# When the convolution taps of a mixer trunk stand in VectorE's queue: taps held back longer, gates spread out, transposed chunks used later, norm steps later

## The chip, the cores and the metric

One core of one Trainium2 chip runs the kernel. The metric is device time in microseconds (us) of one execution. The engines in play are TensorE (PE for its matmuls, PEld for its weight loads), VectorE (DVE), ScalarE (ACT), GpSimd (POOL) and SyncE (SP). Each takes its instructions in the order in which they stand in its queue, so an instruction that waits holds up everything behind it on that engine. For this kernel a difference of about 0.3% is what can be told from no change.

## The reference, cut to what matters

Two layers (DEPTH = 2) run over 256 tokens of width 2048. Each layer normalises x, multiplies it with one wide input projection, feeds three branches from it, and merges them:

```
h = rms_norm(x, norm_w);  proj = h @ w_in
qa, ka, va, za, qi, ki, wi, ub, zb, qc, kc, vc, zc, gates = split(proj)
y_a = (dsa_attention(rope(qa), rope(ka), va, rope(qi), rope(ki), wi, top_k=64) * silu(za)) @ w_a_out
y_b = (conformer_conv(ub) * silu(zb)) @ w_b_out   # GLU, depthwise causal conv of 31 taps, LayerNorm, swish
y_c = (stick_breaking_attention(qc, kc, vc) * silu(zc)) @ w_c_out
x   = x + (g_a*y_a + g_b*y_b + g_c*y_c) @ w_out   # g = sigmoid(gates)
```

After the second layer a final RMSNorm gives the output. All is float32. The 1024 convolution channels are 8 blocks of 128, so a layer has 8 x 31 = 248 tap instructions of 128x256 elements.

## The kernel before, in words

**Weight units.** Every large product is fed by weight units of half a megabyte, mostly 2 x 128 rows by 512 columns (`load_unit`, L193). A unit is loaded into `raw` (4 buffers) by a DMA that SP issues; ACT rounds it to `wh` (`high`, L216; the cast of L218); DVE forms the rest `wl = raw - wh` (`low`, L220; the subtraction of L222). Both `wh` and `wl` have 3 buffers. PE then does 8 matmuls with `wh` and 4 with `wl` for a unit (L232). So DVE may run ahead of PE by less than three units, and whatever else DVE does must fit between two subtractions of L222, or PE waits for `wl`.

**Shapes of chunk.** `chunk_N` (L332) makes 512 output columns by tokens in 8 units; `chunk_T` (L235) makes two heads of features by tokens in 4 units (the 16 index query heads, called QI here, take 8 such chunks, and `rope`, L383, works on each). `chunk_F` (L286) is a `chunk_N` whose result is turned by `turned` (L254): DVE transposes 32x32 blocks, POOL issues four DMAs to a scratch tensor `z` and, two units later, one DMA back into `zy`; the result is used `later` units after the chunk.

**Order.** The program is written in one order with priorities, and a list scheduler in the recording layer orders each engine's instructions from it. `high`, `low` and the loads have high priority. Several devices place side work between units: `waiting` holds convolution taps in items of one or two, and `drain` (L174) puts one item after each `low`, tied to stand behind that subtraction, unless `hold[0]` is set; `flush` (L185) emits all that is left in `waiting` at once, tied to nothing; `stages` holds generators (index scores, attention, stick breaking, the convolution's norm) of which `background` (L156) advances one per unit, and `finish` runs them out; `pending` holds the turned results and `settle` runs them out.

**Taps.** `use_u` (L672) copies a turned half of the GLU output (4 channel blocks) to `yT` on ACT and calls `taps` (L661), which puts the taps of that half in `waiting`: channel blocks two at a time, their taps alternating, so that neighbours in the queue write different rows of `cv`. `hold[0]` is set before the QI chunks (L698) and cleared behind them (L702). `tap` (L420) is one VectorE instruction, L424 for the first tap of a block and L426 for the other 30; each of these reads and writes its block of `cv`.

**The layer's sequence.** Two chunks of the first product with the squares and the norm's factor beside them (`chunk_first`, `start_0`, `start_1`, `follow`); the second half of the GLU; QI, KI, VA with the index weights, KA; QA (two `chunk_F` with `rope_F`) and QC (two) with the index scores and the choice of the top 64 as stages; KC, VC with attention as stages; the gate ZA; then for the branches in the order A, C, B four rounds of a gate chunk (8 units) and an output chunk (4 units). The gates ZC and ZB stand just ahead of branches C and B. `conv_norm` (L909) starts in branch C at j = 2, after a `flush`: it sums `cv` over the channels (L914, L915), PE forms the mean (L918), DVE subtracts it (L921), ACT squares, DVE sums again (L924, L925), PE forms the variance (L928), and so on; it gives 3 units between the first two steps and 6 before the variance. Last come the output product and, for layer 0, the transposes of the last x tile for the next layer (`x_turn`, L435, called at L633).

Of the kernel before, what the change touches and what calls it, by code (L numbers as in the profile page):

```python
# [14 lines left out]
P = 128  # L15
S = 256
NT = S // P
# [7 lines left out]
TOPK = 64  # L25
TAPS = 31
PRE = 2
LATER = 9
URGENT = 10 ** 6
PAD = TAPS - 1  # L30
EPS = 1e-6
# [17 lines left out]
def trunk(ctx: ExitStack, tc: tile.TileContext, x, w_in, xt, w_a, w_b, w_c, w_out,  # L49
# [235 lines left out]

    def chunk_F(w, c0, act, nk, use, later=LATER):  # L286
        turned(chunk_N(w, [(c0, 512)], act, nk), use, later)
# [121 lines left out]
    def gate(c0, o, b, w, hx):  # L409
        def use(k, y):  # L410
            sg = sigmoid_of(y)
            yield 1
            nc.vector.tensor_mul(y, y, sg)  # L413
            nc.vector.tensor_mul(y, y, blocks(o[:, k:k + 4, :]).rearrange("p k u i -> p u k i"))
            split(blocks(hi(b, k, 4)), blocks(lo(b, k, 4)), by_feature(y))

        for k in range(0, KC, 4):
            chunk_F(w, c0 + k * P, hx, KD, partial(use, k), LATER - 1)

    def tap(yT, cv, pr, c, q):  # L420
        wq = pr[:, P_CW + c * TAPS + q:P_CW + c * TAPS + q + 1]
# [52 lines left out]
    for layer in range(DEPTH):  # L474
# [8 lines left out]
        with tc.manual_schedule(engines={nc.vector.engine}), ExitStack() as order:  # L483
# [11 lines left out]
            def low_x(i):  # L495
                k = i * 2
                xs = xT[k // KC][:, k % KC:k % KC + 2, :]
                nc.vector.tensor_sub(lo(hx, k, 2), xs, hi(hx, k, 2).bitcast(F32))
# [8 lines left out]

            def follow(k0):
                u = k0 // 2
                if u:  # L510
                    scale_x(u - 1)
                if u > 1:
                    low_x(u - 2)
                if u == 3:
                    for t in range(NT):
                        nc.scalar.activation(sgs[t], ga[t], AF.Sigmoid, scale=state["r"][:, t:t + 1])
                return advance_units(k0)[0], None if u else lambda: spread(state["dg"])

            todo = [(k, 2, seg[0]) for k in range(0, KD, 2)] + [(k, 2, seg[1]) for k in range(0, KD, 2)]
            loaded, ready = [], []  # L520
# [72 lines left out]
            def start_0(k0):  # L593
                if k0 == 0:
                    load(2)
                    warm_sqrt()
                    load_x(2)
                    load()
                    load_x(4)
                    load()  # L600
                    ps = mm_tile()
                    for _ in range(10):
                        nc.tensor.matmul(ps[:, :P], idle, idle, start=True, stop=True)
                    nc.vector.tensor_copy(loaded[0][1], loaded[0][0])
                    x_high(0)
                    high(loaded[1])
                    x_low(0)
                    for u in loaded[:2]:
                        low(u)
                    ready.extend(loaded[:2])  # L610
                    del loaded[:2]

                    def between():
                        step(2)
                        load_x(6)
                        load()

                    return next_unit(0) + next_unit(1), between
                if k0 < 14:
                    step(k0 + 2)  # L620
                    if k0 < 10:
                        load_x(k0 + 6)
                    load()
                    return next_unit(k0), None
                sq = state["sq"]
                state["sum"] = state["sq2"][:, :S]
                nc.vector.tensor_add(sq[:, :2 * S], sq[:, :2 * S], sq[:, 2 * S:])
                nc.vector.tensor_add(state["sum"], sq[:, :S], sq[:, S:2 * S])
                return advance_units(k0)[0], total_square

            def start_1(k0):
                if k0 == 2:
                    x_parts(x_turn(tail), xn, 12, nw, 4)  # L633
                if k0 == 14:
                    state["r"] = rsqrt_mean(ssq_total(ssq), D)
                    state["dg"] = diag_cols(state["r"])
                return advance_units(k0)
# [8 lines left out]
            order.close()  # L646
            ua = chunk_first(ux, follow)
        with tc.high_priority():
            scale_x(KD // 2 - 1)
            low_x(KD // 2 - 2)  # L650
            low_x(KD // 2 - 1)
        if layer == 0:
            for d, v in ((upper_r, upper), (ones_r, ones)):
# [34 lines left out]
        with tc.high_priority():  # L688
            for t in range(NT):
                nc.vector.tensor_mul(sgs[t], a[t], sgs[t])  # L690
        turned(sgs, partial(use_u, 1), LATER + 2)


        qi = [slot(F32R).rearrange("p a b -> p (a b)").rearrange("p (h t) -> p h t", t=P) for _ in range(2)]
# [4 lines left out]
        for h in range(0, NIH, 2):  # L699
            rope(chunk_T(w, O_QI + h * P, 256, hx, KD, TOPK), qi0[:, h * TOPK:h * TOPK + P].rearrange("p (h t) -> p h t", h=2),  # L700
                 tuple(v[:, h:h + 2, :] for v in qi))
        hold[0] = False  # L702
        kiT = sp.tile([P, 1, S], F32, tag="kiT", bufs=1, name=nm("kiT"))
        rope(chunk_T(w, O_KI, P, hx, KD), kiT)
        with tc.high_priority():
# [89 lines left out]
        for h in range(0, NH, 4):  # L795
            chunk_F(w, O_QC + h * P, hx, KD, partial(use_q, h))
        finish()

        def attend(t, c, qaT=qaT, kaT=kaT, va=va, bias=bias):
            n = (t + 1) * P  # L800
# [34 lines left out]
                start(attend(t, c))  # L835


        kcT, vc = slot(), slot()

        def use_k(h, y, kcT=kcT):  # L840
            nc.scalar.copy(blocks(kcT[:, h:h + 4, :]), by_feature(y))
# [1 line left out]

        for h in range(0, NH, 4):
            chunk_F(w, O_KC + h * P, hx, KD, partial(use_k, h))
        vcr = vc.rearrange("p a b -> p (a b)").rearrange("p (t f) -> p t f", t=NT)
        for j in range(2):
            a = chunk_N(w, [(O_VC + j * 512, 512)], hx, KD)
# [52 lines left out]
                                 lb[:, 512 + q * P:512 + (q + 1) * P], start=False, stop=True)  # L901
            nc.scalar.copy(qcT[:, h0:h0 + 2, :], po[:, :512].rearrange("p (h t) -> p h t", h=2))

        ga = parts(KC)
        gate(O_ZA, qaT, ga, w, hx)
        for h0 in range(0, NH, 2):
            start(stick(h0))

# [38 lines left out]
            yield 0  # L947

        for b in (0, 2, 1):
            if b == 2:  # L950
                finish()
                settle()
                gc = parts(KC)
                gate(O_ZC, qcT, gc, w, hx)
            if b == 1:
                finish()
                settle()
                gb = parts(KC)
                gate(O_ZB, cv, gb, w, hx)
                mx = parts(KD)  # L960
            gx = ga if b == 0 else gc if b == 2 else gb
            for j in range(4):
                if b == 2 and j == 2:
                    finish()
                    flush()
                    start(conv_norm())
                g = chunk_N(w, [(O_G + b * D + j * 512, 512)], hx, KD)
                sg = [ev() for _ in range(NT)]
                with tc.high_priority():
                    for t in range(NT):  # L970
                        nc.scalar.activation(sg[t], g[t], AF.Sigmoid)  # L971
                if j == 0:
                    settle()
                y = chunk_N((w_a, w_b, w_c)[b][layer], [(j * 512, 512)], gx, KC)
                with tc.high_priority():
                    for t in range(NT):
                        dst = mg[j // 2][:, j % 2, t, :]
                        if b == 0:
                            nc.vector.tensor_mul(dst, y[t], sg[t])
                        else:  # L980
                            nc.vector.tensor_mul(sg[t], y[t], sg[t])  # L981
                            nc.vector.tensor_add(dst, dst, sg[t])  # L982
                if b == 1:
                    turned([mg[j // 2][:, j % 2, t, :] for t in range(NT)], partial(use_m, j))


        last = layer == DEPTH - 1
# [21 lines left out]
        def emit_x(xc, accs, q, c0, ts):  # L1009
# [10 lines left out]
            else:  # L1020
                x_squares([xc[:, t, :] for t in ts], ssq, q, ts)
                if q < 3:
                    turned([xc[:, t, :] for t in ts], partial(x_parts_F, xn, c0 // P, nwn), LATER - 1,
                           t4() if q == 1 else None)

        def store_x(xc, c0):
# [103 lines left out]
```

## Time and profile before

| what | value |
|---|---|
| median of 3 runs | 2044.97 us (2043.63 to 2049.26) |
| the profiled execution's own time | 2046.64 us |
| its span, first to last instruction | 2044.9 us |
| mean granted TensorE clock | 0.999 |
| PE busy | 2030.1 us, 99% of the span |
| DVE busy | 1492.4 us, 73% |
| ACT busy | 1039.8 us, 51% |

The profile shows one execution. The span lies 1.7 us under that execution's time. The ends of matmuls are modelled, so a busy PE may still be paced by gaps between matmul starts: where PE is 99% busy, the distance from one group's start to the next, and the number of matmuls in a stretch, say more than the busy time. In the timeline view a row is: start, us, engine, line and operation, output<-input and shapes, and how many were merged; the square bracket gives the idle time before it and what ended that.

### The profile page before, as it was taken

The numbers are of one execution on the slowest core, as the hardware profiler recorded it, in microseconds if no ns is written. First come the engines' busy times: TensorE is split into PE (matmuls) and PEld (weight loads), VectorE is DVE, ScalarE is ACT, GpSimd is POOL, SyncE is SP. The second block draws the span as 40 slices with busy tenths as digits, with TensorE's granted clock in tenths as the row PEclk, the third lists the DMA queues.
The fourth block names the chain that finished last, engine by engine and source line by source line (L and its number), as shares of the span: only waits on it lengthen the run. The fifth ranks groups of instructions, "written<-read, shape, count | busy, mean of one in ns | idle before, by whom it ended". The sixth has DMA issues, their size and how long they took to land.

```text
span 2044.9 us, 26156 instructions
## 1 busy us (share of the span) xinstructions
PE 2030.1 (99%) x9680; PEld 1716.5 (84%) x9680; DVE 1492.4 (73%) x2020; ACT 1039.8 (51%) x1223; POOL 119.4 (6%) x199
## 2 busy tenths in 40 slices
PE   9999999999999999999999999999999999999998
PEld 7899888888888888888888998888888888878887
DVE  8678988688778675655775799886886676656565
ACT  7465445466444454444554654554664444544443
POOL 0100011010000001010100001110100000011000
PEclk9999999999999999999999999999999999999999
DMA  7777587675567667776877776776756776677774
GB/s 258 230 243 213 161 244 210 200 221 167 178 199 228 185 198 227 241 234 213 295 212 231 229 198 178 238 212 192 222 163 180 212 215 195 187 235 244 244 225 152
DMA packets 246528, 435.03 MB, mean 213 GB/s; under 512 B 19712, under 2 KB 69888, under 8 KB 246272
## 3 DMA queue, kind: packets, MB, share of 16 engines
q1 hardware_dynamic: 231632, 389.32, 63.1%
q0 software_dynamic: 13104, 40.91, 6.5%
q10 hardware_dynamic: 1664, 3.15, 0.4%
q8 instruction: 75, 1.23, 0.2%
q14 instruction: 53, 0.43, 0.1%
HBM read 408.67 MB, written 24.64 MB: 212 GB/s over the span
## 4 chain that ended last, share of the span: by engine, by line
PE 92%; DVE 3%; DMA 2%; issue 1%; ACT 1%; POOL 0%; SPq 0%; DVEq 0%; ACTq 0%; POOLq 0%
PE acc L232 89%; DMA zy<-z 1%; DVE wl L222 1%; DMA z<-zt 1%; PE mm L771 1%; PE mm L804 1%; ACT wh L218 0%; PE mm L829 0%; DVE s L426 0%; PE mm L898 0%; PE mm L862 0%; DMA raw<-in_w_in_dram 0%; DVE sc L730 0%; POOL z L268 0%; PE mm L821 0%
## 5 line engine op out<-in xcount | busy, mean ns | idle before, releaser
L232 PE MATMUL acc<-wh,s 128*128 128x512 f32 (+2 forms) x5248 | 1284.5, 387 | 3.3 <-ACT wh L218 3.3
L222 DVE TENSOR_TENSOR wl<-raw,wh 128x1024 fp32r<-128x1024 f32 (+2 forms) x729 | 875.2, 1206 | 400.5 <-ACT wh L218 399.6
L218 ACT CAST wh<-raw 128x1024 fp32r<-128x1024 f32 (+2 forms) x728 | 756.5, 1043 | 785.6 <-PE acc L232 532.4
L232 PEld LDWEIGHTS acc<-wh,s 128*128 128x128 f32 x5248 | 970.7, 188 | 200.0 <-ACT wh L218 5.3
L232 PE MATMUL acc<-wl,s 128*128 128x512 f32 (+2 forms) x2624 | 692.4, 386 | 0.7 <-DVE wl L222 0.7
L232 PEld LDWEIGHTS acc<-wl,s 128*128 128x128 f32 x2624 | 486.9, 188 | 102.6 <-DVE wl L222 4.1
L426 DVE SCALAR_TENSOR_TENSOR s<-yT,cst,s 128x256 f32<-128x256 f32 x480 | 216.1, 476 | 0.5
L268 POOL DMA_DIRECT2D z<-zt x152 | 88.8, 591 | 1639.4 <-DVE zt L265 1491.3
L232 PE MATMUL acc<-s,wh 128*128 128x384 f32 (+1 forms) x608 | 125.6, 348 | 0.0
L232 PEld LDWEIGHTS acc<-s,wh 128*128 128x128 f32 x608 | 104.3, 189 | 3.2
L232 PEld LDWEIGHTS acc<-s,wl 128*128 128x128 f32 x608 | 79.1, 191 | 0.9
L232 PE MATMUL acc<-s,wl 128*128 128x192 f32 (+1 forms) x608 | 79.4, 273 | 0.0
L366 ACT CAST s<-zy 128x1024 fp32r<-128x1024 f32 x20 | 21.0, 1050 | 46.6 <-DMA zy<-z 29.1
L367 DVE TENSOR_TENSOR s<-zy,s 128x1024 fp32r<-128x1024 f32 x20 | 24.4, 1218 | 27.7 <-ACT s L366 27.7
L273 POOL DMA_DIRECT2D zy<-z x39 | 28.0, 719 | 201.3 <-DMA z<-zt 112.4
L265 DVE STREAM_TRANSPOSE zt<-acc 128x512 f32<-128x512 f32 x48 | 34.0, 708 | 7.2 <-PE acc L232 7.2
L981 DVE TENSOR_TENSOR ev<-acc,ev 128x512 f32<-128x512 f32 x32 | 22.0, 687 | 19.1 <-PE acc L232 19.1
L391 DVE TENSOR_TENSOR ev<-ev,cst 128x384 f32<-128x384 f32 (+2 forms) x20 | 11.1, 557 | 25.0 <-ACT ev L389 24.9
L406 ACT ACTIVATE t<-zy 128x1024 f32<-128x1024 f32 x12 | 12.7, 1061 | 29.5 <-DMA zy<-z 29.5
L413 DVE TENSOR_TENSOR zy<-zy,t 128x1024 f32<-128x1024 f32 x12 | 14.6, 1220 | 16.4 <-ACT t L406 16.4
L971 ACT ACTIVATE ev<-acc 128x512 f32<-128x512 f32 x48 | 26.3, 590 | 0.0
L982 DVE TENSOR_TENSOR s<-s,ev 128x512 f32<-128x512 f32 x32 | 21.8, 682 | 0.0
(206 smaller groups left out, 822.5 us busy)
## 6 DMA issues: line engine op xcount, KB each, us to landing
raw<-in_w_in_dram SPq DMA_DIRECT2D x555, 512.0 KB, 3.9
raw<-in_w_out_dram SPq DMA_DIRECT2D x64, 512.0 KB, 4.9
zy<-z POOLq DMA_DIRECT2D x39, 512.0 KB, 5.2
z<-zt POOLq DMA_DIRECT2D x152, 128.0 KB, 4.4
raw<-in_w_a_dram SPq DMA_DIRECT2D x32, 512.0 KB, 3.9
raw<-in_w_c_dram SPq DMA_DIRECT2D x32, 512.0 KB, 4.7
raw<-in_w_b_dram SPq DMA_DIRECT2D x32, 512.0 KB, 5.4
raw<-in_w_in_dram SPq DMA_DIRECT2D x16, 256.0 KB, 3.0
```

The costliest lines, as they stand in the source:

```text
L218: newest_parts[0] = nc.scalar.copy(u[1], u[0])
L222: newest_parts[1] = sub = nc.vector.tensor_sub(u[2], u[0], u[1].bitcast(F32))
L232: newest[0] = nc.tensor.matmul(o, lhsT, rhs, start=start, stop=stop, skip_group_check=True)
L265: nc.vector.transpose(tmp[:, t].rearrange("p b k i -> p k b i"), src.rearrange("p (k b c) -> p k b c", b=4, c=32))
L268: nc.gpsimd.dma_start(z[:, :, :, a, :].rearrange("t b c e -> c (t b) e"), tmp[a * 32:(a + 1) * 32].rearrange("c t b k i -> c (t b) (k i)"))
L273: nc.gpsimd.dma_start(y.rearrange("p (t a) k i -> p t (a k i)", t=n), z.rearrange("t b c a e -> (b c) t (a e)"))
L366: nc.scalar.copy(h, src)
L367: nc.vector.tensor_sub(l, src, h.bitcast(F32))
L426: nc.vector.scalar_tensor_tensor(o, yT[:, c, q:q + S], wq, o, op0=ALU.mult, op1=ALU.add)
L971: nc.scalar.activation(sg[t], g[t], AF.Sigmoid)
L981: nc.vector.tensor_mul(sg[t], y[t], sg[t])
L982: nc.vector.tensor_add(dst, dst, sg[t])
```

## The change

It has these parts.

1. **Taps.** `hold[0] = False` moves from behind the QI chunks to behind the `finish()` after the QC chunks, so `drain` gives out no taps in between.
2. **Later uses.** LATER goes from 9 to 11. A turned chunk is used two units later, but for the merged tiles and x tiles, whose `later` is lowered by two so that it stays, and `use_u(1)`, which stays at 11. `gate` uses 10 and 12.
3. **Gates spread out.** The gate ZA moves from behind VC to between KC and VC, with a `finish()` ahead of it; ZC moves into branch A at j = 3; ZB moves into branch C at j = 3, behind a `finish()`. `flush` and the start of `conv_norm` move from branch C, j = 2, to j = 1.
4. **Norm steps later.** In layer 0 the square sum's product (`total_square`) moves from the last unit of the first chunk into the first unit of the second; `spread`, `scale_x`, `low_x` and the sigmoid of `ga` move one unit later in both layers; in layer 1 the transposes of the last x tile move from k0 = 2 to k0 = 6.

```diff
-LATER = 9
+LATER = 11
...
-            chunk_F(w, c0 + k * P, hx, KD, partial(use, k), LATER - 1)
+            chunk_F(w, c0 + k * P, hx, KD, partial(use, k), LATER + 1 if k else LATER - 1)
...
-                if u:
-                    scale_x(u - 1)
                 if u > 1:
-                    low_x(u - 2)
-                if u == 3:
+                    scale_x(u - 2)
+                if u > 2:
+                    low_x(u - 3)
+                if u == 4:
...
-                return advance_units(k0)[0], None if u else lambda: spread(state["dg"])
+                root = total_square if layer == 0 else None
+                return advance_units(k0)[0], root if u == 0 else (lambda: spread(state["dg"])) if u == 1 else None
...
-                return advance_units(k0)[0], total_square
+                return advance_units(k0)
...
-                if k0 == 2:
+                if k0 == 6:
                     x_parts(x_turn(tail), xn, 12, nw, 4)
...
-        turned(sgs, partial(use_u, 1), LATER + 2)
+        turned(sgs, partial(use_u, 1))
...
-        hold[0] = False
         kiT = sp.tile([P, 1, S], F32, tag="kiT", bufs=1, name=nm("kiT"))
...
         finish()
+        hold[0] = False
...
             chunk_F(w, O_KC + h * P, hx, KD, partial(use_k, h))
+        finish()
+        ga = parts(KC)
+        gate(O_ZA, qaT, ga, w, hx)
+        vc = slot()
...
-        ga = parts(KC)
-        gate(O_ZA, qaT, ga, w, hx)
...
-            if b == 2:
-                finish()
-                settle()
-                gc = parts(KC)
-                gate(O_ZC, qcT, gc, w, hx)
             if b == 1:
-                finish()
-                settle()
-                gb = parts(KC)
-                gate(O_ZB, cv, gb, w, hx)
                 mx = parts(KD)
...
-                if b == 2 and j == 2:
+                if b == 0 and j == 3:
                     finish()
+                    gc = parts(KC)
+                    gate(O_ZC, qcT, gc, w, hx)
+                if b == 2 and j == 1:
                     flush()
                     start(conv_norm())
+                if b == 2 and j == 3:
+                    finish()
+                    gb = parts(KC)
+                    gate(O_ZB, cv, gb, w, hx)
...
-                    turned([mg[j // 2][:, j % 2, t, :] for t in range(NT)], partial(use_m, j))
+                    turned([mg[j // 2][:, j % 2, t, :] for t in range(NT)], partial(use_m, j), LATER - 2)
...
-                    turned([xc[:, t, :] for t in ts], partial(x_parts_F, xn, c0 // P, nwn), LATER - 1,
+                    turned([xc[:, t, :] for t in ts], partial(x_parts_F, xn, c0 // P, nwn), LATER - 3,
```

The scheduler's order of the changed program can be read without running it. In VectorE's queue of layer 0, between the 43rd and the 51st subtraction L222 (in the QI chunks; wl marks such a subtraction, counted as unit 43, 44 and so on, "tap" stands for L424 or L426, the numbers for other lines, which are those of the kernel before):

```
unit 43 wl | tap x2 | unit 44 wl | 293 | tap x3 | 391 392 | unit 45 wl | 401 398 | tap x2 | 367 | tap x2 |
unit 46 wl | tap x6 | unit 47 wl | tap x6 | unit 48 wl | 293 | tap x4 | 391 392 | unit 49 wl |
401 398 | tap x2 | 367 | tap x2 | unit 50 wl | tap x2 | unit 51 wl
```

These are 31 taps: one L424 and 30 L426, neighbours tied by a semaphore to each other: the taps of one whole channel block. In the program before there is no tap at this place. The same stands in layer 1. Around the start of `conv_norm` the changed order of VectorE is (E marks the unit whose matmuls stand just ahead of the mean product L918 in PE's queue):

```
tap x4 | wl of E | tap x3 | wl of E+1 | tap x2 | 914 | wl of E+2 | 915 | 921 | wl of E+3 | 921 | wl of E+4 | 924 924 | wl of E+5 | 925
```

and PE's: unit E but for its last matmul, 918, that matmul, units E+1, E+2 and E+3, one matmul of unit E+4, 928. The last 31 taps, which stand from nine units ahead of E to E+2, are again of one block. In the program before the last tap stands three units ahead of the first L914, and L918 stands 18 units behind the second.

More of the change, by code (lines that the diff above doesn't have):

```diff
@@ L648, in trunk @@
         with tc.high_priority():
-            scale_x(KD // 2 - 1)
-            low_x(KD // 2 - 2)
+            for i in (2, 1):
+                low_x(KD // 2 - i - 1)
+                scale_x(KD // 2 - i)
             low_x(KD // 2 - 1)
@@ L835, in trunk @@
                 start(attend(t, c))
-        kcT, vc = slot(), slot()
+        kcT = slot()
         def use_k(h, y, kcT=kcT):
```

## The prediction

> **What bounds the kernel now.** I read the page's busy times first, then PE's waits, then the windows view, then the timelines of the stretches that the change touches.
>
> ```profile
> span 2044.9 us, 26156 instructions
> PE 2030.1 (99%) x9680; PEld 1716.5 (84%) x9680; DVE 1492.4 (73%) x2020; ACT 1039.8 (51%) x1223; POOL 119.4 (6%) x199
> PEclk9999999999999999999999999999999999999999
> ```
>
> PE is busy for 99% of the span at the full granted clock, and the change adds and removes no matmul. So it can only fill PE's gaps or open new ones. Where are the gaps? The windows view gives each stretch's length, then busy time and instruction count of PE, PEld, DVE, ACT and POOL:
>
> ```profile
> 242.00:275.00 33.00, 32.18 (x138) 24.98 (x137) 31.83 (x61) 14.02 (x15) 3.05 (x5) 1.00 0.68 208
> 1255.00:1288.00 33.00, 31.81 (x136) 24.78 (x135) 31.41 (x61) 13.99 (x14) 3.06 (x5) 1.00 0.70 211
> 560.00:593.00 33.00, 33.00 (x147) 27.36 (x146) 23.29 (x34) 13.64 (x14) 0.00 (x0) 1.00 0.67 195
> 535.00:680.00 145.00, 145.00 (x641) 120.10 (x640) 103.28 (x129) 63.69 (x64) 6.10 (x10) 1.00 0.69 206
> ```
>
> Undisturbed, PE puts 147 matmuls through in 33 us, and over 145 us one in 145 / 641 = 0.226 us. Where the index scores' top 64 are chosen, with taps beside them, it is 138 and 136, and DVE is busy for 31.8 and 31.4 of 33 us. 138 x 0.226 = 31.2 and 136 x 0.226 = 30.8 us are work; 1.8 and 2.2 us are lost, **4.0 us** over both layers. The other gaps that the change touches are small:
>
> ```profile
> PE mm L589 <- DVE t L628: 1.2, 1, 1.2
> ```
>
> ```profile
> 1022.74 0.33 PE L440 MATMUL mm<-cst,t 128*128 128x128 f32 x1
> 1023.34 0.98 PE L440 MATMUL mm<-cst,t 128*128 128x128 f32 x7 [0.27 <-DVE t L1013]
> ```
>
> PE waits 1.2 us for the square sum in layer 0, and the second transpose of the last x tile starts 0.60 us behind the first where the seven others take 0.98 together: 0.5 us lost.
>
> **The change part by part: what goes.** The same window for L426 alone (DVE's time, then taps):
>
> ```profile
> 242.00:275.00 33.00, 7.80 (x17) 1.00 0.68 208
> ```
>
> Without these 7.8 us DVE's 31.8 of 33 become 24, so its lateness goes. Part of the same loss is another wait that the later uses remove: the rotation's copy L374 holds ACT until its chunk has landed, with the next cast behind it.
>
> ```profile
> 270.59 1.05 ACT L374 COPY t<-zy 64x1024 f32<-64x1024 f32 x1 [5.14 <-DMA zy<-z]
> 1284.46 1.05 ACT L374 COPY t<-zy 64x1024 f32<-64x1024 f32 x1 [4.62 <-DMA zy<-z]
> ```
>
> Two units more are about 5.4 us, as long as those waits. So I take the 4.0 us as gone. The square sum's product gets 2.7 us more of matmuls ahead of it and loses its 1.2; the factor behind it then has as many matmuls as before to hide under, and the scaling of x is one unit later, still ahead of the units that read it. The transposes of x move 7 us behind their data: 0.5 goes. Sum of gains: **5.7 us**. The gates' moves put each gate 20 units ahead of its use, which costs nothing; POOL's order of transfers stays. Attention's last two steps now stand with one unit between them (the new `finish()`); by the subtractions that stand ahead of theirs in DVE's queue they are ready about when PE asks: 0 to 1 us a layer, taken as 0.
>
> **What comes, first place: the QI chunks.** The changed order has 31 taps of one block between units 43 and 51. They come from the `flush`: draining starts later and stops earlier, so about 61 taps are left there; `flush` ties them to nothing, and the scheduler puts the last block at the first place where its input exists. That input is ACT's copy L673. The stretch as it stands:
>
> ```profile
> 114.13 1.04 ACT L673 COPY yT<-zy 128x1024 f32<-128x1024 f32 x1
> ```
>
> ```profile
> 117.52 1.03 PE L232 MATMUL acc<-s,wl 128*128 128x192 f32 x8
> 118.38 1.59 PE L232 MATMUL acc<-s,wh 128*128 128x384 f32 x8
> 119.81 1.03 PE L232 MATMUL acc<-s,wl 128*128 128x192 f32 x8
> ```
>
> ```profile
> 112.03 3.49 DVE L222 TENSOR_TENSOR wl<-raw,wh 128x1024 fp32r<-128x1024 f32 x3
> 115.58 0.56 DVE L293 TENSOR_TENSOR ev<-acc,ev 128x384 f32<-128x384 f32 x1
> 117.73 0.56 DVE L391 TENSOR_TENSOR ev<-ev,cst 128x384 f32<-128x384 f32 x1 [1.59 <-ACT ev L389]
> 118.20 0.55 DVE L392 TENSOR_TENSOR ev<-ev,cst 128x384 f32<-128x384 f32 x1
> 118.67 1.22 DVE L222 TENSOR_TENSOR wl<-raw,wh 128x1024 fp32r<-128x1024 f32 x1
> 119.81 0.28 DVE L401 TENSOR_TENSOR s<-ev,ev 128x128 f32<-128x128 f32 x1
> 120.01 0.42 DVE L398 TENSOR_TENSOR ev<-ev,ev 128x256 f32<-128x256 f32 x1
> 120.90 0.43 DVE L367 TENSOR_TENSOR s<-ev,s 128x256 fp32r<-128x256 f32 x1 [0.47 <-ACT s L366]
> 121.24 3.49 DVE L222 TENSOR_TENSOR wl<-raw,wh 128x1024 fp32r<-128x1024 f32 x3
> ```
>
> PE takes a unit each 2.29 us (117.52 to 119.81). DVE's costs from start to start are 1.14 for a subtraction, 0.47 for L293, L391 and L392, 0.20 for L401, 0.34 for L398 and L367. A tap's cost depends on what stands ahead of it:
>
> ```profile
> 207.79 1.52 DVE L777 SCALAR_TENSOR_TENSOR sc<-t,sm,sc 128x256 f32<-128x256 f32 x3
> 270.34 1.27 DVE L426 SCALAR_TENSOR_TENSOR s<-yT,cst,s 128x256 f32<-128x256 f32 x3
> ```
>
> Three taps on alternating blocks take 1.27 us, 0.40 from start to start; three L777, same operation and size, each reading what the last one wrote, 1.52, thus 0.52. The trace has no chain of taps; I take L777's pace, the same dependence, so n taps in a row cost 0.52(n - 1) + 0.40. [...]
>
> The copy ends at 115.17; two taps and the subtraction of unit 44 end at about 117.2, 2.6 us ahead of PE's need at 119.81. Then DVE needs, unit by unit: 45: 0.47 + 1.44 + 0.94 + 1.14 = 3.99 (the three taps fill the 1.59 us of idle time); 46: 0.54 + 0.92 + 0.34 + 0.92 + 1.14 = 3.86; 47 and 48: 3.00 + 1.14 = 4.14 each; 49: 0.47 + 1.96 + 0.94 + 1.14 = 4.51; 50: 3.86. That is 24.5 against PE's 6 x 2.29 = 13.7. Less the 2.6 ahead, PE loses 8.2 us. Units 53 and 54, with the next rotation and DVE not yet ahead again, add about 0.7: **8.9 us a layer, 17.8 in all**. At 0.40 a tap it is 5.9 a layer, and with 0.52 for every tap 9.9; I keep both ends.
>
> **Second place: the start of the convolution's norm.** The mean's product L918 now stands in PE's queue before DVE can have its input, and everything of PE is behind it.
>
> ```profile
> 659.44 0.69 DVE L981 TENSOR_TENSOR ev<-acc,ev 128x512 f32<-128x512 f32 x1 [1.31 <-PE acc L232]
> 660.05 1.22 DVE L222 TENSOR_TENSOR wl<-raw,wh 128x1024 fp32r<-128x1024 f32 x1
> ```
>
> ```profile
> 663.78 1.07 PE L232 MATMUL acc<-wl,s 128*128 128x512 f32 x4
> 664.68 1.98 PE L232 MATMUL acc<-wh,s 128*128 128x512 f32 x8
> 666.50 1.07 PE L232 MATMUL acc<-wl,s 128*128 128x512 f32 x4
> ```
>
> ```profile
> 649.73 2.04 DVE L914 TENSOR_REDUCE t<-s 128x256 f32<-128x1024 f32 x1
> 704.29 2.34 DVE L921 TENSOR_TENSOR s<-s,mm 128x1024 f32<-128x1024 f32 x2
> 707.68 3.94 DVE L924 TENSOR_REDUCE t<-t 128x256 f32<-128x1024 f32 x2
> 712.67 0.42 DVE L925 TENSOR_TENSOR t<-t 128x256 f32<-128x256 f32 x1
> ```
>
> A unit takes PE 2.72 us here (663.78 to 666.50). At the end of an output chunk DVE waits for PE (L981) and then delivers the third unit's `wl` at 661.3, 5.2 us ahead of 666.5; with three taps more ahead of L981 I put the lead at 3.7. The units after it cost DVE 2.4 to 3.1 us (a subtraction and 2 to 4 chained taps, 0.92 to 1.96) against 2.72, so it stays near 3.7 up to unit E. From there DVE needs three taps 1.44, a subtraction 1.14, two taps 0.92, L914 1.96, a subtraction 1.14, L915 0.34: 6.9 us. PE reaches L918 0.7 us into unit E's `wl`: it waits 6.9 - 3.7 - 0.7 = 2.5 us. From the mean to the variance DVE needs L921, subtraction, L921, subtraction (4 x 1.14), two L924 (3.9), a subtraction and L925: 10.3 us with a third for the mean product; PE has three units and two matmuls, 8.8: 1.5 us. Together **4.0 us a layer, 8.0 in all**; with a lead of 5.2 it is 2.5, with none 7.7.
>
> **Sum.** 17.8 + 8.0 - 5.7 = +20.1 us. On the profiled execution: 2044.9 + 20.1 = 2065.0 for the span, 2046.64 + 20.1 = 2066.7 for its own time. That execution lies 1.7 us above the median 2044.97, so a median of runs comes out at **2065.0 us**, 1.0% slower.
>
> **The rivals.**
>
> *Faster: DVE swallows the early taps.* The mechanism is the idle time of DVE in the QI chunks, which decides if it and the lead hold all 31 taps; then the norm's product must also find its input.
>
> ```profile
> 100.00:136.00 36.00, 36.00 (x252) 36.00 (x252) 25.73 (x36) 23.68 (x32) 2.77 (x5) 1.00 0.82 248
> ```
>
> Of 36 us 10.3 are idle, 29%; in the eight units that is 5.2 us, and the lead before the copy is 119.81 - 115.52 = 4.3. These 9.5 us hold 18 taps in a chain. All 31 would need 16, at 0.40 still 12.4. If it did, only the gains would be left: 2044.97 - 5.7 = 2039.3. Chance 3%.
>
> *No change.* At the least, 12.4 - 9.5 = 2.9 us a layer are lost in QI, and if the norm's wait were all covered, 5.8 us of loss meet 5.7 of gain: 2045. Chance 6%.
>
> *Slower by less.* Chained taps at 0.40: 2 x 5.9 + 2 x 2.5 - 5.7 = +11.1: 2056. Chance 14%.
>
> *Slower by more: the clock drops.* PE would now idle in bursts; a clock halved for 16 us behind them (seven units of 2.29) would cost 8 us more a layer: 2081. Against it: with 1.8 and 2.2 us lost around 242 and 1255 the clock stayed at 1.00. [...] Chance 5%.
>
> **How the numbers follow.** The forecast has the remaining 72%. Its bounds: low, QI at 5.9 and the norm at 2.5 (+11.1, 2056); high, 9.9 and the norm's 5 (+24.1, 2069), with up to 2 for attention's last steps and 2.5 more for a norm with no lead. I give 2054 to 2074. A difference of 0.3% (6.1 us) is about what can be told from no change: slower beyond it 72 + 14 + 5 = 91%, within it 6%, faster 3%.
>
> **What would show each step right or wrong.** In the changed profile: the QI stretch near 120 to 140 us with DVE busy throughout, PE waiting for `wl` some 1 to 2 us in each of about five units, and the same 1.0 ms later; taps in a chain 0.52 apart; waits of PE at the mean and variance products (2.5 and 1.5); 147 matmuls in 33 us where the top 64 are chosen; no wait at L589. I am wrong if PE keeps its 2.29 us a unit there, or if the wait at the mean's product is absent.

## The result, and the profile after

The changed kernel takes 2061.88 us (median of 6, 2060.94 to 2062.61) against 2045.18 for the kernel before (median of 6, 2043.37 to 2049.26): 1.0079 times, 95% interval 1.0066 to 1.0092, 16.7 us slower. The forecast was 2065.0. The profiled span grows from 2044.9 to 2060.8 us. In the changed file some lines have moved: the mean product is L922 (was L918), the variance product L932 (L928), their inputs L919 and L929; L222, L232 and L426 stay.

The page's first rows, then PE's waits (in total, times, longest):

```profile
span 2060.8 us, 26151 instructions
PE 2035.9 (99%) x9680; PEld 1721.7 (84%) x9680; DVE 1504.4 (73%) x2020; ACT 1042.1 (51%) x1223; POOL 119.2 (6%) x199
```

```profile
PE acc L232 <- DVE wl L222: 10.3, 9, 1.9
PE mm L932 <- DVE t L929: 2.8, 2, 1.4
PE mm L922 <- DVE t L919: 2.3, 2, 1.2
```

DVE's and PE's shares of the span are as before. The waits are what differs: nine for `wl` and four for the norm's products; L589 and ACT's `wh` are gone from the list. The windows view, where the top 64 are chosen (later in the program now):

```profile
258.00:291.00 33.00, 33.00 (x147) 27.32 (x146) 24.25 (x23) 14.90 (x15) 6.09 (x10) 1.00 0.83 252
1273.00:1306.00 33.00, 33.00 (x147) 27.35 (x146) 25.33 (x36) 16.85 (x16) 4.55 (x8) 1.00 0.74 233
```

147 matmuls in 33 us in both layers, where there were 138 and 136. The price stands in the QI chunks. PE's timeline of layer 0, first and last row and those with a wait, then three rows of DVE:

```profile
116.17 1.03 PE L232 MATMUL acc<-s,wl 128*128 128x192 f32 x8
...
123.80 1.14 PE L232 MATMUL acc<-s,wl 128*128 128x192 f32 x8 [0.58 <-DVE wl L222]
...
127.93 1.14 PE L232 MATMUL acc<-s,wl 128*128 128x192 f32 x8 [1.57 <-DVE wl L222]
...
132.07 2.02 PE L232 MATMUL acc<-s,wl 128*128 128x192 f32 x8 [0.56 <-DVE wl L222]
...
140.41 1.14 PE L232 MATMUL acc<-s,wl 128*128 128x192 f32 x8 [1.28 <-DVE wl L222]
...
147.39 1.07 PE L232 MATMUL acc<-s,wl 128*128 128x192 f32 x8
```

```profile
116.32 1.51 DVE L426 SCALAR_TENSOR_TENSOR s<-yT,cst,s 128x256 f32<-128x256 f32 x3
...
123.66 3.08 DVE L426 SCALAR_TENSOR_TENSOR s<-yT,cst,s 128x256 f32<-128x256 f32 x6
126.66 1.22 DVE L222 TENSOR_TENSOR wl<-raw,wh 128x1024 fp32r<-128x1024 f32 x1
```

From unit 43 (116.17) to unit 50 (140.41) are 24.24 us where seven units of 2.29 take 16.0: 8.2 lost. Six taps and the start of the next instruction are 3.00 us apart (123.66 to 126.66), a tap 0.50 to 0.52. The brackets in PE's rows add up to 4.0 us only: the modelled end of a group lies behind the normal start of the next (118.38 + 1.59 = 119.97 against a start at 119.81 in the kernel before), and for part of this stretch the granted clock is 0.50 (the 2.02 us of the row at 132.07 are 1.03 elsewhere; last section). So the distance between starts is the measure.

Where all of the time went, I read from the starts of PE's matmuls: grouped by line, operands and shape, each distance to the next start against its group's median, and the excess summed by stretch (us lost, before to after):

| stretch | layer 0 | layer 1 | change | forecast |
|---|---|---|---|---|
| norm steps | 1.6 to 0.2 | 0.8 to 0.0 | -2.2 | -1.7 |
| QI chunks | 0.4 to 8.8 | 0.4 to 10.6 | +18.6 | +17.8 |
| choice of the top 64 | 2.1 to -0.1 | 2.5 to 0.0 | -4.7 | -4.0 |
| convolution's norm | 0.3 to 3.2 | 0.3 to 3.2 | +5.8 | +8.0 |
| gate ZB's use, end of branch B | 0.6 to -0.2 | 1.7 to -0.2 | -2.7 | not in it |

Together +14.8 of the span's 15.9.

### The profile page after: what moved, and what is told of

Read it like the earlier page. It is cut to its first block, busy times and chain, and to the rows that moved or that the text cites. A ratio compares the mean times of both kernels' runs of the same rounds, so it can differ in the third digit from the quotient of the medians.

```text
span 2060.8 us, 26151 instructions
## 1 busy us (share of the span) xinstructions
PE 2035.9 (99%) x9680; PEld 1721.7 (84%) x9680; DVE 1504.4 (73%) x2020; ACT 1042.1 (51%) x1223; POOL 119.2 (6%) x199
## 4 chain that ended last, share of the span: by engine, by line
PE 94%; DVE 4%; issue 1%; ACT 0%; DVEq 0%; ACTq 0%
PE acc L232 90%; DVE wl L222 2%; DVE s L426 2%; PE mm L772 1%; PE mm L806 1%; PE mm L831 0%; PE mm L904 0%; PE mm L868 0%; PE mm L823 0%; PE mm L604 0%; DVE t L928 0%; PE mm L890 0%; PE mm L743 0%; PE mm L871 0%; PE mm L906 0%
## 5 line engine op out<-in xcount | busy, mean ns | idle before, releaser
L232 PE MATMUL acc<-wh,s 128*128 128x512 f32 (+2 forms) x5248 | 1283.6, 387 | 0.0
L222 DVE TENSOR_TENSOR wl<-raw,wh 128x1024 fp32r<-128x1024 f32 (+2 forms) x729 | 876.6, 1207 | 426.9 <-ACT wh L218 420.5
L232 PEld LDWEIGHTS acc<-wh,s 128*128 128x128 f32 x5248 | 971.0, 188 | 195.1 <-ACT wh L218 0.4
L232 PE MATMUL acc<-wl,s 128*128 128x512 f32 (+2 forms) x2624 | 692.2, 386 | 0.0
L232 PEld LDWEIGHTS acc<-wl,s 128*128 128x128 f32 x2624 | 487.8, 188 | 99.2
L426 DVE SCALAR_TENSOR_TENSOR s<-yT,cst,s 128x256 f32<-128x256 f32 x480 | 218.8, 478 | 3.0
L232 PE MATMUL acc<-s,wh 128*128 128x384 f32 (+1 forms) x608 | 129.4, 355 | 0.0
L232 PEld LDWEIGHTS acc<-s,wh 128*128 128x128 f32 x608 | 107.7, 194 | 3.2
L232 PEld LDWEIGHTS acc<-s,wl 128*128 128x128 f32 x608 | 80.2, 195 | 15.3 <-DVE wl L222 14.3
L232 PE MATMUL acc<-s,wl 128*128 128x192 f32 (+1 forms) x608 | 82.4, 279 | 10.4 <-DVE wl L222 10.3
L388 ACT COPY ev<-ev 64x384 f32<-64x384 f32 (+2 forms) x20 | 10.2, 511 | 25.9 <-DVE ev L293 25.7
L1016 DVE TENSOR_TENSOR t<-acc,t 128x512 f32<-128x512 f32 (+1 forms) x18 | 10.6, 627 | 13.8 <-PE acc L232 13.8
```

Of the source, the lines that this page charges most:

```text
L222: newest_parts[1] = sub = nc.vector.tensor_sub(u[2], u[0], u[1].bitcast(F32))
L232: newest[0] = nc.tensor.matmul(o, lhsT, rhs, start=start, stop=stop, skip_group_check=True)
L426: nc.vector.scalar_tensor_tensor(o, yT[:, c, q:q + S], wq, o, op0=ALU.mult, op1=ALU.add)
```

## The experiments

**Do the leftover taps cost it?** `e1_tied` ties what the flush gives out to the newest subtraction; `e2_hold_back` undoes part 1 alone.

```diff
         while waiting:
-            for f in waiting.pop(0)[1]:
-                f()
+            with tc.issue_after(newest_parts[1].ins):
+                for f in waiting.pop(0)[1]:
+                    f()
```

> The changed kernel, but the taps that flush gives out are tied to stand behind the newest subtraction L222, so the 31 taps of one channel block leave the QI chunks and go behind the flush in branch C, four to a unit over about 25 units; the mean product of the convolution's norm moves 8 units later with them. Theory (the taps in the QI chunks cost 8 to 10 us a layer; 8.4 is read from PE's unit starts in layer 0, about 9.8 from the gaps of layer 1): 2061.9 - 18 = 2044, and with four taps and a subtraction a unit (4 x 0.40 + 1.14 = 2.74 us of VectorE against TensorE's 2.72) nothing new is lost but the norm's two waits of 2.9 us a layer, which stay: 2043 to 2047 us, and the QI chunks back at one unit in 2.29 us. Rival (the later uses of turned chunks, whose copies now stand among the QI chunks, cost the time there): 2058 us or more, with waits for wl in the QI chunks as they are.

Measured: 2043.05 us (10 runs), span 2041.2; 0.9979 of before (0.9970 to 0.9988). The QI chunks are back at a loss of 0.5 us a layer by the same sum. The norm's waits stay (L923 and L933 are its two products in that kernel):

```profile
PE mm L933 <- DVE t L930: 2.8, 2, 1.4
PE mm L923 <- DVE t L920: 1.4, 2, 0.7
```

The theory holds; the later uses, which are all in this kernel, cost nothing in the QI chunks.

```diff
+        hold[0] = False
         kiT = sp.tile([P, 1, S], F32, tag="kiT", bufs=1, name=nm("kiT"))
...
         finish()
-        hold[0] = False
```

> The changed kernel with part 1 alone undone: taps are given out again from behind the QI chunks. By the scheduler's order nothing but a few taps is then left at the flush, there is no tap in the QI chunks, and the mean product stands 8 units behind the sum it needs. Theory (both costs of the change come from the taps that are left over): 2061.9 - 18 (QI) - 5.8 (the norm's waits) = 2038, plus between 0 and 4 us for the taps that stand beside the top-64 choice again, the lower part of it if the later uses have removed the wait of L374: 2038 to 2042 us, below the kernel before. Rival (the spread of the gates or the later uses cost time of their own): 2048 us or more.

Measured: 2039.97 us (5 runs), 0.9961 of before (0.9948 to 0.9974); `e2_again`, the same kernel beside the last two below:

> The changed kernel with part 1 alone undone, the same as before, timed beside the other two: span 2037.9 within 1 us, a median of 2039 to 2041 us.

2040.18 us (8 runs, 2039.89 to 2040.35), 0.9974 (0.9964 to 0.9985). No wait in the QI chunks or the norm; what is left stands at the choice:

```profile
242.00:275.00 33.00, 32.78 (x142) 26.00 (x141) 32.93 (x64) 14.29 (x14) 3.05 (x5) 1.00 0.74 222
1255.00:1288.00 33.00, 32.76 (x142) 26.02 (x141) 32.93 (x61) 16.61 (x16) 3.06 (x5) 1.00 0.76 228
```

142 matmuls with the taps beside them, against 138 and 136 before and 147 without taps. The later uses take away about half of the loss there; `n2_later` (below), which has them alone, also shows 142. The missing taps by themselves take away all of it, as `e3_hold_alone` shows next, so the two effects overlap.

**What puts a block into the QI chunks?** `e5_norm_j2` puts flush and norm back from j = 1 to j = 2; `e3_hold_alone` is the kernel before with part 1 alone. In both the flush comes 12 units later, so that every block has given out its first tap before it.

```diff
-                if b == 2 and j == 1:
+                if b == 2 and j == 2:
                     flush()
                     start(conv_norm())
```

> The changed kernel with the flush and the start of the convolution's norm put back from j = 1 to j = 2 of branch C, 12 units later; taps are still held back until the QC chunks are done. Twelve units more give out about 18 taps more, the last block has then given out its first taps and by the scheduler's order nothing stands in the QI chunks. Theory (what decides is that a block is untouched when the flush comes): 18 us come back, the norm's waits stay: 2043 to 2047 us. Rival (what is left over is done early in any case, only fewer taps of it, 13 of 31): the loss in the QI chunks shrinks to about a third, 2050 us.

Measured: 2042.48 us (10 runs), 0.9978 (0.9968 to 0.9987), half a microsecond below the theory's range; the QI chunks lose no more than in the kernel before. The rival (a third of the loss stays) falls: with the last block's first tap given out, none of its taps stands there, where 13 of 31 were expected by the rival.

> The kernel before with part 1 alone: taps held back until the QC chunks are done, all else as before. The flush then stands 12 units later than in the changed kernel, each block has given out its first taps by then, and by the scheduler's order no tap stands in the QI chunks; 4 taps a unit stand behind the flush and the sums end two units behind the place of the mean product in TensorE's queue. Theory (holding the taps back costs much only through a block that is wholly left over): VectorE's lateness beside the top-64 choice goes (-2 to -4 us), the norm's waits come (+2.9 us a layer, 5.8): 2047 to 2049 us. Rival (taps that are held back cost about what they cost in the changed kernel, wherever they land): 2058 us or more. Second rival (the wait at the mean product is covered): 2041 to 2043.

Measured: 2045.66 us (10 runs, 2043.54 to 2052.04), 0.9999 (0.9989 to 1.0009), with a span of 2044.5, below the theory's 2047 to 2049: the choice gave 4.7 us instead of 2 to 4, and the norm took 4.6 instead of 5.8. Nothing new is lost in the QI chunks and nothing at the choice (148 matmuls in 33 us in both layers). That holds although the copy L374 still waits for its transfer there, 9.5 us in three places (10.3 in the kernel before): without taps beside it, that wait costs PE nothing. At the norm 2.3 us more are lost in each layer. Part 1 alone is thus no loss: what it wins at the choice (4.7) the norm takes back (4.6).

The direct test leaves part 1 and the early flush as they are and moves two taps: the first taps of the last two blocks are given out first.

```diff
                         ops.append(partial(tap, yT, cv, pr, c + d, q))
+            if j == 1:
+                ops = ops[2 * TAPS:2 * TAPS + 2] + ops[:2 * TAPS] + ops[2 * TAPS + 2:]
```

> The changed kernel with one pair of taps moved: the first taps of the last two channel blocks are given out ahead of the other two blocks' taps, all else as in the change. By the scheduler's order nothing stands in the QI chunks; the 60 other taps of these blocks follow their first taps at once, four to a unit over some 30 units of the branches A and C, and the sums end 3 units ahead of the mean product's place in TensorE's queue. Theory (a block that is wholly left over is put where its input exists, which its first tap alone decides): the QI chunks go back to 2.29 us a unit and most of the norm's waits go with the leftovers: span 2060.8 - 17.6 - (3 to 5) = 2038 to 2040, a median of 2039 to 2042 us. Rival (four taps and a subtraction, 2.74 us, make VectorE the bound over these units): as above, but 2 to 3 us a layer more, a span of 2043 or more, with TensorE waiting for wl there.

Measured: **2037.68 us** (5 runs, 2037.53 to 2038.00), 0.9961 of before (0.9947 to 0.9975), the lowest time of all kernels here: 24 us below the change. The page's span, PE's waits, a window of the stretch that now holds the taps, and three rows of DVE in it:

```profile
span 2036.2 us, 26155 instructions
```

```profile
PE acc L232 <- ACT wh L218: 1.1, 1, 1.1
PE mm L604 <- DVE eps L71: 1.1, 1, 1.1
```

```profile
535.00:680.00 145.00, 145.00 (x641) 120.09 (x640) 135.96 (x206) 66.82 (x68) 6.09 (x10) 1.00 0.68 202
```

```profile
606.76 1.67 DVE L426 SCALAR_TENSOR_TENSOR s<-yT,cst,s 128x256 f32<-128x256 f32 x4
608.35 1.22 DVE L222 TENSOR_TENSOR wl<-raw,wh 128x1024 fp32r<-128x1024 f32 x1
609.48 1.67 DVE L426 SCALAR_TENSOR_TENSOR s<-yT,cst,s 128x256 f32<-128x256 f32 x4
```

Both waits are the program's start. DVE is busy for 136 of 145 us and PE loses nothing: 641 matmuls, as before. The rival (DVE becomes the bound at four taps a unit) falls: 606.76 to 609.48 is 2.72 us, PE's own pace. The span is 1.8 us below the theory's 2038 to 2040, because all of the norm's waits go, not most of them, and with them the 2.1 us of the clock (last section). No tap stands in the QI chunks. So the untouched block was the cause there. It needs part 1 and the early flush of part 3 together: `e3_hold_alone` has the one, `n4_gates` (below) the other, and neither has a tap in the QI chunks.

**Does the chain's pace matter?** `e7_two_chains` sums the odd taps of the last block in a second tile (`cx`, the rows `x0n` below), so that neighbours alternate. The tap L426 is L430 in that kernel.

```diff
+        if cx is not None and q % 2:
+            o = cx
...
                     flush()
+                    nc.vector.tensor_add(cv[:, KC - 1, :], cv[:, KC - 1, :], cx)
                     start(conv_norm())
```

> The changed kernel, but the last channel block sums its odd taps in a second tile and adds the two once at the end (one first tap, one addition more), so the same 31 taps stand in the QI chunks with neighbours that write different tiles; by the scheduler's order they fill six units there (3, 4, 5, 7, 8, 4) instead of eight. Theory (what stands there is a serial chain at 0.52 us from start to start, where alternating taps go at 0.40): VectorE needs 30 x 0.12 = 3.6 us a layer less in that stretch, all of it on the path: 2061.9 - 7 = 2055 us (2053 to 2057). Rival (the pace has another cause than the dependence): 2061 to 2063.

Measured: 2058.88 us (4 runs), 3.0 less than the change, where 7 were expected: outside the theory, and below the rival's 2061. The profiled execution, with a span of 2056.1 us, is 4.7 below that of the change; its clock stayed at 0.999, while two of the four runs show 0.996 and 2059.4 or more. PE's rows of layer 1, the change first, then this kernel (units 43, 49, 50 and, where shown, 51, then 53):

```profile
1137.97 1.03 PE L232 MATMUL acc<-s,wl 128*128 128x192 f32 x8
...
1158.36 1.14 PE L232 MATMUL acc<-s,wl 128*128 128x192 f32 x8 [1.94 <-DVE wl L222]
...
1162.19 2.02 PE L232 MATMUL acc<-s,wl 128*128 128x192 f32 x8 [0.59 <-DVE wl L222]
...
1166.63 1.12 PE L232 MATMUL acc<-s,wl 128*128 128x192 f32 x8
...
1171.29 1.03 PE L232 MATMUL acc<-s,wl 128*128 128x192 f32 x8
```

```profile
1136.66 1.03 PE L232 MATMUL acc<-s,wl 128*128 128x192 f32 x8
...
1157.05 1.14 PE L232 MATMUL acc<-s,wl 128*128 128x192 f32 x8 [1.56 <-DVE wl L222]
...
1159.62 1.14 PE L232 MATMUL acc<-s,wl 128*128 128x192 f32 x8
...
1166.60 1.03 PE L232 MATMUL acc<-s,wl 128*128 128x192 f32 x8
```

Ten units take 33.3 us in the change and 29.9 here, where 22.9 is the pace: 10.4 against 7.0 lost (layer 0: 147.39 - 116.17 = 31.2, so 8.3, against 7.0). The pace is confirmed, 0.40 from start to start:

```profile
1145.78 0.47 DVE L430 SCALAR_TENSOR_TENSOR x0n<-yT,cst,x0n 128x256 f32<-128x256 f32 x1
1146.17 0.47 DVE L430 SCALAR_TENSOR_TENSOR s<-yT,cst,s 128x256 f32<-128x256 f32 x1
```

At unit 49 both kernels are equally late (20.39 us after unit 43), but here all 31 taps are done by then and in the change 25: the scheduler packed them into six units, so the faster pace shows only in unit 50 (3.83 us in the change, 2.57 here), and there the addition that joins the two sums costs 0.56 us of it (L970, 1157.46 to 1158.01 on DVE). That leaves 1.3 us a layer, not 3.6; the other 2 us in layer 1 are the clock (last section). The step of the theory that failed is "all of it on the path".

**The other parts alone**, each on the kernel before. Part 4 (`n1_norm_steps`):

> The kernel before with part 4 alone (norm steps later). Theory: TensorE's wait for the square sum (1.2 us) and the one between the first two transposes of the last x tile (0.5) go and nothing comes: span 2044.9 - 1.7 = 2043.2, 2043 to 2044 us. Rival (the factor or the scaling of x is late instead): the span stays at 2044.9, with a new wait of TensorE near 30 or 1040 us.

Measured: 2046.09 us (10 runs, 2042.60 to 2050.49), 0.9999 (0.9990 to 1.0009), with a profiled span of 2041.0 us. In that profile both waits of the norm steps are gone and nothing follows them; it is also an execution in which the gate ZB cost nothing (2.3 us in that of the kernel before), so its span lies below the forecast's. The medians are too widely spread to show a gain of 1.7 us.

Part 2 (`n2_later`):

> The kernel before with part 2 alone (later uses of turned chunks). Theory: beside the top-64 choice the copy L374 no longer holds ScalarE, although taps stand there too; the kernel with part 1 undone lost 0.9 us there where the kernel before loses 4.0: -3.1 us. The wait of ScalarE for the second half of the gate ZB (L406 at 1837, 7.46 us, of which TensorE loses 0.5 and 1.5 in the two layers) stays, since the results are run out 8 units behind the gate here in any case: span 2041.8, 2041 to 2043 us. Rival (only without taps does that stretch lose nothing): span 2044 or more. Second rival (the later use alone removes the gate's wait too): span 2039.5.

Measured: 2046.03 us (10 runs, 2044.86 to 2046.50), 0.9993 (0.9979 to 1.0007), with a span of 2044.4: outside the theory. At the choice 2.3 us are won of 3.1, and the gate ZB costs nothing in the profiled execution, as the second rival had it (2.7); but a wait comes that none of them had, of PE at the stick branch. ACT, then PE:

```profile
462.92 1.28 ACT L406 ACT_TABLE_LOAD   x1 [3.42 <-DMA zy<-z]
464.21 1.06 ACT L406 ACTIVATE t<-zy 128x1024 f32<-128x1024 f32 x1
```

```profile
468.91 0.49 PE L884 MATMUL mm<-ph,upper_r 128*128 128x512 f32 x1 [0.46 <-ACT ph L366]
```

With the gate ZA still behind VC, its second half is used later, among the stick branch's steps, and its sigmoid holds ACT (3.42 us for `zy`, a table load of 1.28) ahead of the split that the product L884 needs: 4.6 us more lost between 460 and 660 and the same place of layer 1. So the first rival's number (2044 or more) came by another cause than its own. Part 3 moves that gate away.

Part 3 (`n4_gates`):

> The kernel before with part 3 alone (gates spread out, the norm's start at j = 1). By the scheduler's order all taps are done before the flush (the sums are ready 10 units ahead of the mean product). Theory (the gate's second half is still used 8 units behind its chunk, so ScalarE still waits for it, and only together with the later uses does that wait go): span 2044.9 give or take 0.7, 2044 to 2046 us. Rival (the spread alone removes the gate's wait): span 2042.5. Second rival (the norm started earlier meets taps and makes TensorE wait): span 2047 or more.

Measured: 2049.18 us (10 runs, 2045.98 to 2054.01), 1.0006 (0.9993 to 1.0019). The profiled span, 2047.8, is outside the theory and reaches the second rival's number, but not by its mechanism: PE waits nowhere at the norm. The gate's wait stays, as the theory said, and is longer in the profiled execution; PE's wait of 1.99 us behind it, and the clock that falls to 0.50 after it (last section), make the excess:

```profile
791.35 1.06 ACT L406 ACTIVATE t<-zy 128x1024 f32<-128x1024 f32 x1 [7.92 <-DMA zy<-z]
```

**Can taps be kept from the choice without leftovers?** `b5_hold_top64` gives taps out behind QI, holds them through the two QC chunks, and starts the norm at j = 2:

```diff
+        hold[0] = True
         qcT = slot()
```

> The changed kernel with taps given out from behind the QI chunks, held back only during the two QC chunks (where the top 64 are chosen), and the norm started at j = 2 of branch C again. By the scheduler's order no tap stands in the QI chunks or in the choice, and the sum stands 4 units ahead of the mean product. Theory: against the kernel with part 1 undone (span 2037.9) the 0.9 us that it still loses beside the choice goes and nothing comes: span 2036.5 to 2037.5, a median of 2038 to 2039.5 us. Rival (a lead of 4 units in the queue doesn't cover the norm's products): TensorE waits 0.5 to 1.5 us a layer there, span 2038 to 2040.

Measured: 2040.46 us (9 runs, 2039.75 to 2040.73), 0.9971 (0.9957 to 0.9984). Theory and rival both miss: the norm waits for nothing, and the loss at the choice is as with the taps.

```profile
242.00:275.00 33.00, 32.66 (x142) 26.01 (x141) 29.21 (x50) 15.17 (x15) 4.20 (x7) 1.00 0.78 240
```

In DVE's queue the choice begins near 241 us and taps stand in it up to 248, since they were given out before the QC chunks: DVE's lead is used up by then. It looks as if the hold came one chunk late; no run sets it earlier.

## Why the prediction was right, point by point

- **QI chunks.** Right in place, cause and size: 8.2 us lost by unit 50 in both layers (140.41 - 116.17 and 1162.19 - 1137.97 are both 24.2), the number worked out unit by unit. For units 47 to 50 it had 4.14, 4.14, 4.51 and 3.86 us of DVE's time; PE's units come 4.13, 4.14, 4.50 and 3.84 apart. Of the 0.7 for units 53 and 54 only 0.3 came in layer 0 (140.41 to 149.91 are 9.50 us for four units of 2.29) and nothing in layer 1, where the clock took 2.1 between units 50 and 51 instead. That the total of 18.6 is so near the forecast's 17.8 is in that part luck.
- **The rival with 0.40 a tap** falls: the chain goes at 0.50 to 0.52. Its 5.9 us a layer are not contradicted by the 7.0 of e7, which has that pace: ahead of unit 50's subtraction e7 has two taps more (0.8 us) and the addition L970 (0.56), and without them it would lose about 5.6, an estimate from these rows. The prediction's time for this rival, 2056, has the norm at 5.0; with the forecast's 8.0 there its terms add up to 2059.
- **The norm's products** were mis-sized: waits of 2.5 and 1.5 were forecast, 1.2 and 1.4 came.

```profile
690.02 0.70 PE L922 MATMUL mm<-t,cst 128*128 128x256 f32 x2 [1.16 <-DVE t L919]
...
700.74 0.70 PE L932 MATMUL mm<-t,cst 128*128 128x256 f32 x2 [1.39 <-DVE t L929]
```

  The step at fault is the lead of 3.7 us, lowered from 5.2 for three more taps. The changed profile has the lead at unit E itself, DVE's rows first, then PE's:

```profile
681.75 1.22 DVE L222 TENSOR_TENSOR wl<-raw,wh 128x1024 fp32r<-128x1024 f32 x1
...
689.55 0.41 DVE L919 TENSOR_TENSOR t<-t 128x256 f32<-128x256 f32 x1
```

```profile
688.01 0.84 PE L232 MATMUL acc<-wl,s 128*128 128x512 f32 x3
```

  The subtraction is done at 681.75 + 1.14 = 682.9 and PE starts with it at 688.0: a lead of 5.1. The path behind it was right (682.9 to 689.96, 7.1 against 6.9). The three taps cost the lead next to nothing because DVE had been idle for 1.31 us just there, waiting for PE; the prediction showed that row (L981) and took the taps off the lead all the same. In the change DVE no longer waits at that place.
- **The choice of the top 64**: 4.0 forecast, 4.7 won. The first cause, the taps, suffices (e3). The second, L374's wait, was no part of the loss once the taps were gone; the later uses matter there only while taps stand beside the choice (e2, n2).
- **Norm steps**: 1.7 forecast, 2.2 in the table; they cost PE 1.4 and 0.8 us, where 1.2 and 0.5 were counted.
- **What the prediction did not have** is a gain of 2.7 us at the gate ZB. It costed the gates' moves at nothing. In the kernel before, the sigmoid of the gate's second half stands in ACT's queue before its transfer has landed, with the next cast of `wh` behind it; here ACT and PE of the kernel before, then ACT of the change:

```profile
1837.09 1.06 ACT L406 ACTIVATE t<-zy 128x1024 f32<-128x1024 f32 x1 [7.46 <-DMA zy<-z]
```

```profile
1839.14 2.14 PE L232 MATMUL acc<-wh,s 128*128 128x512 f32 x8 [1.53 <-ACT wh L218]
```

```profile
1828.27 1.06 ACT L406 ACTIVATE t<-zy 128x1024 f32<-128x1024 f32 x1
```

  ACT waits before L406 for 29.5 us in ten places of the kernel before, and nowhere in the change. What of it reaches PE differs from profile to profile at this gate: 0.6 and 1.7 us before, 1.9 and 0.1 in e3, 0 and 0 in n1. The kernels without part 2 also spread over 6 us or more from run to run (before, e3, n1, n4), those with it over 0.3 to 1.7 (the change, e1, e2, e5, e7, e8, b5, n2). Part of the spread goes with the clock: of the 66 runs of the kernel before that were timed beside the experiments, 45 show a mean granted clock of 0.999, with a median of 2045.4 us, 17 show 0.998, with 2048.4, and four show 0.996 or 0.997, with 2050.6 to 2059.0. That L406's waits make the spread, by themselves or through the clock, is an inference; no run took them alone away.
- **The clock** was a rival with 5%, at 8 us a layer. The granted clock did drop to 0.50, but for 6.8 us in each layer (129.15 to 135.96 and 1159.97 to 1166.79 us) instead of the 16 that the prediction assumed, and it cost nothing in layer 0, where DVE was the bound, and 2.1 us in layer 1.

The sum for the span, +20.1, was 4.2 too high (15.9 came): 2.2 at the norm, 2.7 at the gate, 0.7 at the choice and 0.5 at the norm steps, less 0.8 in QI and 1.1 outside the table.

## What to carry to other kernels

Where a list scheduler orders a queue, work that is tied to nothing goes where its first input exists, however long before it is wanted: look at the first instruction of each chain of leftovers, and tie or issue that one. Judge an engine by its lead at the instruction that somebody waits for: DVE at 94% with an even four taps a unit cost nothing, and 31 taps ahead of the wrong subtractions cost 8 us a layer, with DVE's share of the span at 73% in both kernels. Parts of a change may need each other: parts 2, 3 and 4 each alone showed no gain in the medians, while together they gave 5 us (e2 beside the kernel before, 2040.2 against 2045.1) and with well-placed taps 7 (e8, 2037.7).

## What the runs showed of the hardware

The granted clock fell to half amid the kernel without any wait of PE over 2 us (the longest was 1.94 in the change and 1.99 in n4). The windows view of layer 0 of the change:

```profile
126.00:128.00 2.00, 0.43 (x4) 0.11 (x2) 1.96 (x4) 0.00 (x0) 0.00 (x0) 1.00 0.38 134
128.00:130.00 2.00, 2.00 (x12) 2.00 (x13) 1.86 (x5) 0.00 (x0) 0.00 (x0) 0.79 0.44 113
130.00:132.00 2.00, 1.51 (x5) 1.00 (x4) 1.96 (x4) 0.00 (x0) 0.00 (x0) 0.50 0.42 150
132.00:134.00 2.00, 1.93 (x9) 1.93 (x10) 1.89 (x6) 1.45 (x3) 0.00 (x0) 0.50 0.34 86
134.00:136.00 2.00, 2.00 (x8) 2.00 (x8) 2.00 (x4) 0.61 (x1) 0.00 (x0) 0.51 0.51 177
136.00:138.00 2.00, 1.86 (x14) 1.54 (x13) 1.96 (x6) 0.92 (x2) 0.00 (x0) 1.00 0.11 18
```

It stays at half until 136 us; DVE was the bound there anyway (PE's wait at 132.07 is for `wl`). In layer 1 it falls only at 1160 (0.50 from 1160 to 1166 us, 0.80 in 1166 to 1168), when DVE is nearly ahead again: unit 50 takes 4.44 us (1162.19 to 1166.63), 2.1 over its pace, and that is the difference between the layers. In n4 one wait of 1.99 us was followed by it:

```profile
793.39 2.64 PE L232 MATMUL acc<-wh,s 128*128 128x512 f32 x8 [1.99 <-ACT wh L218]
795.83 1.91 PE L232 MATMUL acc<-wl,s 128*128 128x512 f32 x4
```

The four `wl` matmuls take 1.91 us there, 1.07 elsewhere; the granted clock is 0.70 in 794 to 796 us, 0.50 in 796 to 798 and 0.95 in 798 to 800. In e3 a wait of 1.79 us at the gate ZB was not followed by a drop: the eight `wh` matmuls behind it take 2.11 us (825.61), in n4 2.64. In e7 the waits of 1.74 (1152.93) and 1.56 us (1157.05) in the QI chunks were not followed by one either (the `wl` group at 1159.62 takes 1.14 us), while in the change the waits of 1.57 (127.93) and 1.94 us (1158.36) were. So the length of one wait does not tell these cases apart, 1.57 with a drop and 1.79 without; what does is not shown by these runs.

All six runs of the change show a mean clock of 0.996 to 0.998, the profiled runs of e1, e2, e5 and e8 0.999.
